# A two-layer trunk whose first tile after three norms is multiplied in float32 ahead of the norm's factor, and whose output is turned in the kernel

## The chip, the cores and the metric

The kernel runs on one core of a Trainium2 chip. A core has a matrix engine (TensorE, PE in the profile), a vector engine (VectorE, DVE), a scalar engine for activations, copies and casts (ScalarE, ACT), GpSimd (POOL), a queue engine that issues most DMAs (SyncE, SP), and 16 DMA engines. The engines run side by side, each in its own program order, and wait for each other by semaphores. Sums of matmuls stand in PSUM, eight buffers of 128 x 512 float32 here; everything else is in SBUF or, for weights and output, in HBM.

The metric is the device time of one execution in microseconds (us). A version has several executions, and its time is their median. The profile describes one further execution.

## The reference

A decoder trunk of two layers for 256 tokens (T) with 1024 features (D). Layer 0 mixes tokens by attention in three dilated windows, layer 1 by gated linear attention (GLA, in chunks of 64 tokens). Each is followed by a feed-forward part (FFN) with a causal convolution of width 3 and a gate. All of it is float32.

```
for i in range(DEPTH):
    mod = jax.nn.silu(c) @ w_ada[i] + b_ada[i]
    sh1, sc1, g1, sh2, sc2, g2 = [m[:, None, :] for m in jnp.split(mod, 6, axis=-1)]
    h = rmsnorm(x, norm_mix[i]) * (1.0 + sc1) + sh1
    if i % N_MIXERS == 0:
        y = dilated_mixture(h, w_in_a[j], w_out_a[j], rel_bias)
    else:
        y = gla_mixer(h, w_in_b[j], w_gate_b[j], b_gate_b[j], gnorm_b[j], w_out_b[j])
    x = x + g1 * y
    h = rmsnorm(x, norm_ffn[i]) * (1.0 + sc2) + sh2
    x = x + g2 * conv_ffn(h, w_up[i], conv_w[i], conv_b[i], w_down[i])
return rmsnorm(x, norm_final)
```

`rmsnorm(x, g)` is x times the inverse root of its mean square (over the features, plus 1e-6) times g. `conv_ffn` is u = h @ w_up, the convolution of u over the tokens, silu of one half times the other, and @ w_down. In `gla_mixer`, h @ w_in gives q, k, v, a low-rank input of the decay, and r, and the end is (rmsnorm(o, g_norm) * silu(r)) @ w_out.

Written for one token: h @ w = factor * ((x * a) @ w) + shift @ w, where a is the norm's weight times (1 + scale) and the factor is one number for each token.

## The kernel before

Activations lie with features on the partitions: `x` is eight tiles (kt = 0 to 7) of 128 features x 256 tokens. A weight matrix is used in tiles of 128 x 2048 float32, which is 256 output features for all eight kt, or another cut of that size.

**Split products.** A weight tile is loaded by SP into `raw` (four buffers), then `split` (L155) makes two float32r tiles of it: ACT casts it to `whi` (L165, two halves) and DVE subtracts that from `raw` into `wlo` (L168, two halves). Activations are split in the same manner. `mm3` (L171) is three matmuls in float32r, hi x hi (L174), hi x lo (L175) and lo x hi (L176). One tile of w_up, or of a gate, is 8 kt x 2 halves of features x 3 = 48 matmuls of 128x256.

**A norm.** As each tile of x is finished by `residual` (L271, DVE) at the end of a projection, `add_square` (L195) squares it on ACT and adds it to one of three partial sums, on POOL for kt 1 and 2 and else on DVE; kt 7 has a sum of its own. `rstd_of` (L183) sums over the partitions by a matmul with a matrix of 1/1024 (`ms`, L186, float32, three of them), then ACT takes Ln (L188) and Exp (L190): `r`, the factor, the same in all partitions. `all_normed` (L265) puts six small matmuls that nothing reads (`keep_warm`, L259) behind ms, and calls `normed` (L246) for each kt: DVE multiplies x by a and r (`xr`, L250), ACT adds the shift and casts (`hhi`, L252), DVE makes the rest (`hlo`, L253). `chain[kt]` keeps the last two instructions of kt; `chain[7]` those of the latest kt.

**Order.** A scheduler puts the instructions of each engine into one order when the program is built; `with behind(...)` says that what is inside is not issued before the instructions named. What runs on an engine is then fixed. A wait of one instruction holds everything behind it on its engine.

**PSUM.** `bank` (L72) hands out the eight buffers by three tags, p (2 buffers), s (3) and t (3). Without a tag it takes the next letter of `"pstpstst"`, round and round. A buffer is written again only after its readers are done.

**FFN** (L539): 22 tiles of w_up (`pab`, both halves of the gated pair in one buffer), convolution on ACT and DVE out of PSUM, and the split of the product; then w_down (`pd`). The split of tile 0 may begin from the sixth square on, that of tile 1 from `chain[3]` on, the others from `chain[7]`.

**GLA** (L592 to L781): norm, values (`pv`, L649 to L660), decay gates, then for each of four heads `states` (L671) and `output` (L716), and between the outputs the four gate tiles (`gate`, L741, matmuls `pr`), gate 0 ahead of the last output and gates 1 to 3 behind it. Then per head silu of the gate (L770), the product (L774), its split (`ohi` L776, `olo` L777), and `project` (L515, matmuls `py`).

```
    s3 = states(3)
    output(2, *s2)
    gate(0)
    next_ada()
    output(3, *s3)
    for n in range(1, 4):
        gate(n)
```

**The end** (L785 to L792): the last norm has no split. Its factor is multiplied into x by two multiplies on POOL and six on DVE, and four DMAs write 256 KB each, features on the partitions; the host turns the result.

**Modulation.** `next_ada` (L351) computes two of the 96 columns of shift, scale and gate at a time: a DMA of 1 MB, two dot products on DVE (L138). They are strewn over the program.

Of the kernel before, what the change touches and what calls it, by code (L numbers as in the profile page):

```python
# [57 lines left out]
def trunk(ctx: ExitStack, tc: tile.TileContext, I, out):  # L58
# [136 lines left out]
    def add_square(kt):  # L195

        sq = tmp.tile([P, T], F32, tag="sq", name="sq")
        i = nc.scalar.activation(sq, x[kt], AF.Square)
# [152 lines left out]
    def next_ada():  # L351
        if rest:
            ada_chunk(*rest.pop(0))
# [181 lines left out]
    project(I["w_out_a"], o, 0, 0)  # L535
    at_pool.__exit__(None, None, None)


    def ffn(l):  # L539
        h = all_normed(l, 1)  # L540
        with tc.tile_pool(name=f"ffn{l}", bufs=2) as pool:
            g_hi = [pool.tile([P, T], F32R, tag=f"ghi{i}", name="ghi", bufs=1) for i in range(NFF)]
            g_lo = [pool.tile([P, T], F32R, tag=f"glo{i}", name="glo", bufs=1) for i in range(NFF)]
            for i in range(NFF):
                with behind(*(squared[:1], chain[3], chain[7])[min(i, 2)]):
                    w = split(I["w_up"][l, i], 2048)
                pab = bank("pab")
                pu = [pab[:, :T], pab[:, T:]]
                for kt in range(KT):
                    for s in range(2):  # L550
                        mm3(pu[s][:, :T], parts(w, 2 * P * kt + P * s), h[kt], kt == 0 and s == 0, kt == KT - 1 and s == 1)
# [21 lines left out]
            exp_ln_after(silu)  # L573
            for f2 in range(0, KT, 2):
                pd = [bank("pd") for _ in range(2)]
                for half, f in ((0, 0), (0, 1), (1, 0), (1, 1)):
                    w = split(I["w_down"][l, f2 + f, half], 11 * P)
                    for j in range(11):
                        i = 11 * half + j
                        mm3(pd[f][:, :T], parts(w, P * j), (g_hi[i], g_lo[i]), i == 0, i == NFF - 1)  # L580
                for f in range(2):
                    residual(l, 1, f2 + f, pd[f][:, :T])
                    add_square(f2 + f)
                    if l == 1 and f2 + f < KT - 1:
# [4 lines left out]
    ffn(0)  # L589

# [11 lines left out]
    nc.gpsimd.memset(keep.rearrange("p (n c) -> p n c", c=CH)[:, :, 0:1], 0.0)  # L602
    h = all_normed(1, 0)

# [45 lines left out]
    for n in range(4):  # L650
        with behind(*(squared, chain[5], chain[7], glr_copy)[n]):
            w = split(I["w_v_b"][n], 2048)
            if n > 1:
                next_ada()
        for i in range(2):
            kt = 2 * n + i
            for t in range(2):
                ht = [y[:, P * t : P * t + P] for y in h[kt]]
                for s in range(2):
                    mm3(pv[t][s], ht, parts(w, D * i + 512 * s, 512), kt == 0, kt == KT - 1)  # L660
        if n == 1:
            e_q, e_k, e_d, dec = log_gates()
# [75 lines left out]

    r_g = []

    def gate(n):  # L741
        w = split(I["w_r_b"][n], 2048)
        pr = bank("pr", "p")
        for kt in range(KT):
            for s in range(2):
                mm3(pr[:, T * s : T * s + T], parts(w, 2 * P * kt + P * s), h[kt],
                    kt == 0 and s == 0, kt == KT - 1 and s == 1)
        if n % 2 == 0:
            r_g.append(gt([P, 4, T], "r4", tag=("C", "cs")[n // 2]))
        nc.scalar.copy(r_g[-1][:, 2 * (n % 2) : 2 * (n % 2) + 2, :], pr.rearrange("p (a b) -> p a b", a=2))  # L750

# [6 lines left out]
    output(2, *s2)  # L758
    gate(0)
    next_ada()  # L760
    output(3, *s3)
    for n in range(1, 4):
        gate(n)
        if n < 2:
            next_ada()
    o = []
    for n in range(4):
        r = r_g[n // 2][:, 2 * (n % 2) : 2 * (n % 2) + 2, :]
        with behind(*norm_ops):
# [9 lines left out]
    exp_ln_after(last_hi)  # L779
    project(I["w_out_b"], o, 1, 0)  # L780
    gl_pool.__exit__(None, None, None)  # L781

    ffn(1)

    r = rstd_of([sums[0], sums[1], sums[2]])  # L785
    for kt in range(2):
        nc.gpsimd.tensor_tensor(x[kt], x[kt], r, op=ALU.mult)
    for kt in range(2, KT - 1):
        nc.vector.tensor_tensor(x[kt], x[kt], r, op=ALU.mult)
    nc.vector.scalar_tensor_tensor(x[7], x[7], col(C_NFIN + 7), r, op0=ALU.mult, op1=ALU.mult)  # L790
    for eng, a, b in ((nc.sync, 2, 4), (nc.scalar, 0, 2), (nc.sync, 4, 6), (nc.sync, 6, 8)):
        eng.dma_start(out[a:b].rearrange("k p t -> p k t"), x_all[:, a:b, :])  # L792

# [77 lines left out]
def build(arrays):  # L871
    import concourse.bacc as bacc

    nc = bacc.Bacc("TRN2", target_bir_lowering=False, num_devices=1)
# [4 lines left out]
    out = nc.dram_tensor("out_y", (KT, P, T), F32, kind="ExternalOutput").ap()  # L879
    with tile.TileContext(nc, schedule_with_timeline_sim=True) as tc:  # L880
# [12 lines left out]
```

## Time and profile before

| | us |
|---|---|
| median of three runs | 809.89 |
| the runs | 803.45, 811.63, 809.89 |
| the profiled execution | 807.78 |
| its span on the engines | 806.1 |
| PE busy in it | 782.4 |
| DVE busy in it | 645.4 |
| ACT busy in it | 466.5 |
| mean granted clock of PE in it | 0.993 |

The span is the time from the first to the last instruction; the 1.7 us beside it lie around the program. Rows of the timeline have the start in us from the span's start, the length (of several instructions of one kind in a row together), engine, line, operation, output<-inputs by the program's names, their shape and count, and in brackets how long the engine had been idle and what ended that. The length of a matmul includes its way through the array, so matmuls overlap, and the distance of their starts is what one costs in a stream. A float32 matmul shows as two records, a float32r one as one.

### The profile page before, as it was taken

What the parts mean: (1) busy time and instruction counts of PE and PEld (TensorE: products, weight loads), DVE (VectorE), ACT (ScalarE), POOL (GpSimd) and SP (SyncE); (2) the same over time, 40 slices, a digit from 0 to 9 for tenths busy, and PEclk for the clock granted to TensorE, in tenths of its full rate; (3) what the DMA queues carried; (4) which work ended last, traced back from release to release, by engine and by line L of the source; (5) the groups of instructions that cost most, each with busy time, mean ns of one, the idle gap of its engine ahead of it and who ended that gap; (6) DMA issues with size and microseconds to landing.
All of it is one profiled execution on the core that took longest, in us unless ns stands there. A gap on an engine that the chain in (4) does not pass through costs nothing.

```text
span 806.1 us, 15899 instructions
## 1 busy us (share of the span) xinstructions
PE 782.4 (97%) x6464; PEld 752.5 (93%) x6464; DVE 645.4 (80%) x1153; ACT 466.5 (58%) x867; POOL 16.8 (2%) x42
## 2 busy tenths in 40 slices
PE   8999999999999989999999999999999999999995
PEld 6899999999999889999999998889998999999995
DVE  6998977879778769999997877776468999987552
ACT  5566555455545547777766445644556866766551
POOL 1000000000000010000000000000010000000100
PEclk9999999999999999999999999999999999999998
DMA  8998668486596736877647884873343776644521
GB/s 343 416 328 320 225 256 309 164 305 237 205 321 224 262 105 215 313 257 261 222 136 244 285 322 151 327 261 105 105 159 107 281 274 237 252 145 146 188 99 52
DMA packets 32694, 184.70 MB, mean 229 GB/s; under 512 B 5804, under 2 KB 8364, under 8 KB 15982
## 3 DMA queue, kind: packets, MB, share of 16 engines
q1 hardware_dynamic: 32350, 183.44, 63.1%
q8 instruction: 50, 0.82, 0.4%
q10 hardware_dynamic: 272, 0.26, 0.1%
q14 instruction: 22, 0.18, 0.1%
HBM read 182.59 MB, written 1.10 MB: 228 GB/s over the span
## 4 chain that ended last, share of the span: by engine, by line
PE 67%; DVE 14%; DMA 11%; ACT 4%; issue 2%; DVEq 0%; SPq 0%; ACTq 0%
PE pab L176 10%; PE pab L174 10%; PE pab L175 10%; DVE wlo L168 6%; DMA raw<-in_wqk 5%; PE pd L176 4%; PE pd L175 4%; PE pd L174 4%; PE pqk L176 3%; PE pqk L175 3%; PE pqk L174 3%; DMA raw<-in_wv 2%; DVE ada_raw L138 2%; PE py L175 2%; PE py L174 2%
## 5 line engine op out<-in xcount | busy, mean ns | idle before, releaser
L168 DVE TENSOR_TENSOR wlo<-raw,whi 128x1024 fp32r<-128x1024 f32 (+2 forms) x274 | 295.3, 1106 | 56.9 <-ACT whi L165 56.0
L165 ACT CAST whi<-raw 128x1024 fp32r<-128x1024 f32 (+2 forms) x274 | 247.9, 953 | 153.9 <-PE pab L175 50.5
L174 PE MATMUL pab<-hhi,whi 128*128 128x256 f32 x704 | 194.1, 277 | 1.5 <-ACT hhi L252 1.5
L175 PE MATMUL pab<-hlo,whi 128*128 128x256 f32 x704 | 193.9, 276 | 0.5 <-DVE hlo L253 0.5
L176 PE MATMUL pab<-hhi,wlo 128*128 128x256 f32 x704 | 194.0, 276 | 0.4 <-DVE wlo L168 0.4
L174 PEld LDWEIGHTS pab<-hhi,whi 128*128 128x128 f32 x704 | 132.0, 188 | 2.2 <-ACT hhi L252 1.9
L175 PEld LDWEIGHTS pab<-hlo,whi 128*128 128x128 f32 x704 | 132.0, 188 | 0.9 <-DVE hlo L253 0.9
L176 PEld LDWEIGHTS pab<-hhi,wlo 128*128 128x128 f32 x704 | 132.0, 188 | 0.8 <-DVE wlo L168 0.8
L174 PE MATMUL pqk<-hhi,whi 128*128 128x256 f32 x448 | 123.5, 287 | 3.0 <-ACT hhi L252 2.3
L175 PE MATMUL pqk<-hlo,whi 128*128 128x256 f32 x448 | 125.6, 284 | 0.5 <-DVE hlo L253 0.5
L176 PE MATMUL pqk<-hhi,wlo 128*128 128x256 f32 x448 | 125.0, 283 | 0.0
L138 DVE CUSTOM_DVE_ANT_0 ada_raw<-ada_raw,c_bc 128x1024 f32<-128x1024 f32 x96 | 114.1, 1224 | 5.1 <-DMA ada_raw<-in_w_ada 5.0
L176 PE MATMUL pd<-ghi,wlo 128*128 128x256 f32 x352 | 98.0, 280 | 1.5 <-DVE wlo L168 1.5
L175 PE MATMUL pd<-glo,whi 128*128 128x256 f32 x352 | 98.1, 280 | 0.0
L174 PE MATMUL pd<-ghi,whi 128*128 128x256 f32 x352 | 97.7, 279 | 0.0
L174 PEld LDWEIGHTS pqk<-hhi,whi 128*128 128x128 f32 x448 | 83.7, 191 | 4.7 <-ACT hhi L252 2.7
L175 PEld LDWEIGHTS pqk<-hlo,whi 128*128 128x128 f32 x448 | 85.4, 191 | 1.0 <-DVE hlo L253 0.7
L176 PEld LDWEIGHTS pqk<-hhi,wlo 128*128 128x128 f32 x448 | 85.1, 191 | 0.2
L176 PEld LDWEIGHTS pd<-ghi,wlo 128*128 128x128 f32 x352 | 65.8, 187 | 1.7 <-DVE wlo L168 1.7
L175 PEld LDWEIGHTS pd<-glo,whi 128*128 128x128 f32 x352 | 66.0, 188 | 0.0
L174 PEld LDWEIGHTS pd<-ghi,whi 128*128 128x128 f32 x352 | 65.9, 188 | 0.0
L558 ACT ACTIVATE r<-pab,small 128x256 f32<-128x256 f32 x88 | 48.5, 559 | 11.7 <-DVE r L561 11.3
(176 smaller groups left out, 1247.0 us busy)
## 6 DMA issues: line engine op xcount, KB each, us to landing
ada_raw<-in_w_ada SPq DMA_DIRECT2D x47, 1024.0 KB, 6.5
raw<-in_w_up SPq DMA_DIRECT2D x44, 1024.0 KB, 5.1
raw<-in_w_down SPq DMA_DIRECT2D x32, 704.0 KB, 4.2
raw<-in_wqk SPq DMA_DIRECT2D x18, 1024.0 KB, 7.0
raw<-in_wv SPq DMA_DIRECT2D x14, 768.0 KB, 4.6
raw<-in_w SPq DMA_DIRECT2D x7, 960.0 KB, 6.6
raw<-in_w_out_a SPq DMA_DIRECT2D x4, 1024.0 KB, 6.4
raw<-in_w_v_b SPq DMA_DIRECT2D x4, 1024.0 KB, 5.7
```

Of the source, the lines that this page charges most:

```text
L138: nc.vector.tensor_tensor_reduce(w, w, c_bc, op0=ALU.mult, op1=ALU.add, scale=1.0, scalar=0.0, accum_out=dot,)
L165: copied[0] = nc.scalar.copy(hi[:, c], raw[:, c])
L168: last_lo[0] = nc.vector.tensor_tensor(lo[:, c], raw[:, c], hi[:, c].bitcast(F32), op=ALU.subtract)
L174: mm(ps, a[0], b[0], start=start, stop=False)
L175: mm(ps, a[0], b[1], start=False, stop=False)
L176: return mm(ps, a[1], b[0], start=False, stop=stop)
L558: nc.scalar.activation(r, u[:, :T], AF.Identity, scale=cw[2], bias=col(C_CB + 44 * l + f))
```

## The change

For three of the norms (ahead of both FFNs and of GLA) the tile of weights that came first, or in GLA the tile of gate 0, is not split. It is multiplied in float32 with `early_x` = x times a, which needs no factor. A 257th column of `early_x` holds the shift, so that shift @ w comes out in the 257th column of the sums. Four of the sixteen products (kt 0 and 1) stand ahead of `ms`, twelve behind it, in the place of the small matmuls. When the factor is there, `whole` makes the finished tile of the sums: ACT copies the 257th column, DVE multiplies by the factor, ACT adds the column.

In the FFN, tile 0 of w_up thus has no matmuls of its own; `whole` stands behind `chain[5]`, the split of tile 1 may begin from `chain[0]`, that of tile 2 from `chain[5]`. In GLA gate 0 is made at the norm and kept; gate 1 takes the place that gate 0 had ahead of the last output, and gates 2 and 3 stand behind it. The early sums are in two buffers with tag p in the FFNs and with tag t in GLA. The new instructions are 48 float32 matmuls of 128x257, 24 scalings of x and 24 copies of one column on ACT, and for each of the three tiles two small copies, two multiplies and two additions; 144 split matmuls and three splits go.

At the end, x is turned by 16 transposes on PE into four buffers, the mean square is taken with tokens on the partitions (128 x 4 numbers), the factor is applied by two scalings on ACT and two on DVE out of PSUM, and four DMAs write 128 x 512 each, tokens on the partitions. The host no longer turns the result. A smaller scratch for DMA descriptors makes room in SBUF.

```diff
@@ add_square, norms
-            (nc.gpsimd if kt < 3 else nc.vector).tensor_tensor(acc, sums[part], sq, op=ALU.add)
+            last_sum[:] = [(nc.gpsimd if kt < 3 else nc.vector).tensor_tensor(acc, sums[part], sq, op=ALU.add)]
-    def all_normed(l, sub):
-        r = rstd_of([sums[0], sums[1], sums[2]])
+    early_x = [state.tile([P, T + 16], F32, tag=f"ex{k}", name="early_x") for k in range(KT)]
+    def shift_columns(l, sub):
+        with behind(*chain[7]):
+            for kt in range(KT):
+                nc.scalar.copy(early_x[kt][:, T : T + 1], mod[l, 3 * sub, kt])
+    def scale(l, sub, kt):
+        return nc.scalar.mul(early_x[kt][:, 0:T], x[kt], mod[l, 3 * sub + 1, kt][:, 0:1])
+    def load_early(src):
+        early = wraw.tile([P, 2048], F32, tag="raw", name="raw")
+        nc.sync.dma_start(early, src)
+        return early
+    def all_normed(l, sub, tag, early):
+        ps = [bank("early", tag) for _ in range(2)]
+        def products(tiles):
+            for kt in tiles:
+                for s in range(2):
+                    mm(ps[s][:, 0 : T + 1], early[:, 2 * P * kt + P * s : 2 * P * kt + P * s + P], early_x[kt][:, 0 : T + 1],
+                       start=(kt == 0), stop=(kt == KT - 1))
+        products(range(2))
+        r = rstd_of([sums[0], sums[1], sums[2]], tag="t" if tag == "p" else "s")
         with behind(norm_ops[0]):
-            keep_warm(6)
-        return [normed(l, sub, r, kt) for kt in range(KT)]
+            products(range(2, KT))
+        def whole(s, out):
+            dot = tmp.tile([P, 1], F32, tag="dot", name="dot", bufs=4)
+            nc.scalar.copy(dot, ps[s][:, T : T + 1])
+            nc.vector.tensor_tensor(out, ps[s][:, 0:T], r, op=ALU.mult)
+            nc.scalar.activation(out, out, AF.Identity, bias=dot[:, 0:1])
+            return out
+        return [normed(l, sub, r, kt) for kt in range(KT)], whole
     def residual(l, sub, kt, ps):
-        i = nc.vector.scalar_tensor_tensor(x[kt], ps, g[:, 0:1], x[kt], op0=ALU.mult, op1=ALU.add)
+        with behind(*(last_sum if kt == 7 else ())):
+            i = nc.vector.scalar_tensor_tensor(x[kt], ps, g[:, 0:1], x[kt], op0=ALU.mult, op1=ALU.add)
@@ project (and likewise at w_down of the first FFN, with w_r_b[0])
+        shift_columns(l, 1)
...
+            if n == 3:
+                early = load_early(I["w_up"][l, 0])
             for i in range(2):
                 residual(l, sub, 2 * n + i, ps[i][:, T * i : T * i + T])
                 add_square(2 * n + i)
+                scale(l, 1, 2 * n + i)
@@ ffn
-                with behind(*(squared[:1], chain[3], chain[7])[min(i, 2)]):
-                    w = split(I["w_up"][l, i], 2048)
-                pab = bank("pab")
-                pu = [pab[:, :T], pab[:, T:]]
-                for kt in range(KT):
+                if i == 0:
+                    with behind(*chain[5]):
+                        pu = [whole(s, pool.tile([P, T], F32, tag="u", name="u")) for s in range(2)]
+                else:
+                    with behind(*((), chain[0], chain[5], chain[7])[min(i, 3)]):
+                        w = split(I["w_up"][l, i], 2048)
+                    pab = bank("pab")
+                    pu = [pab[:, :T], pab[:, T:]]
+                for kt in range(KT if i else 0):
@@ GLA
-        with behind(*(squared, chain[5], chain[7], glr_copy)[n]):
+        with behind(*(chain[0], chain[5], chain[7], glr_copy)[n]):
             w = split(I["w_v_b"][n], 2048)
...
+        if n == 0:
+            with behind(*chain[5]):
+                r_g = [gt([P, 2, T], "r2")]
+                for s in range(2):
+                    whole(s, r_g[0][:, s, :])
...
-    gate(0)
+    gate(1)
     next_ada()
     output(3, *s3)
-    for n in range(1, 4):
+    for n in range(2, 4):
         gate(n)
@@ the end
-    r = rstd_of([sums[0], sums[1], sums[2]])
-    for kt in range(2):
-        nc.gpsimd.tensor_tensor(x[kt], x[kt], r, op=ALU.mult)
-    for kt in range(2, KT - 1):
-        nc.vector.tensor_tensor(x[kt], x[kt], r, op=ALU.mult)
-    nc.vector.scalar_tensor_tensor(x[7], x[7], col(C_NFIN + 7), r, op0=ALU.mult, op1=ALU.mult)
-    for eng, a, b in ((nc.sync, 2, 4), (nc.scalar, 0, 2), (nc.sync, 4, 6), (nc.sync, 6, 8)):
-        eng.dma_start(out[a:b].rearrange("k p t -> p k t"), x_all[:, a:b, :])
+    halves = [slice(P * t, P * t + P) for t in range(2)]
+    y_ps = [[bank("y") for _ in range(2)] for _ in halves]
+    ps = bank("ms")
+    nc.vector.tensor_scalar(x[7], x[7], col(C_NFIN + 7), None, op0=ALU.mult)
...
+    for half in range(2):
+        for t, own in enumerate(halves):
+            c = slice(512 * half, 512 * half + 512)
+            d = y[:, D * t : D * t + D][:, c]
+            if t:
+                nc.vector.tensor_scalar(d, y_ps[t][half], r[:, 2:3], None, op0=ALU.mult)
+            else:
+                nc.scalar.mul(d, y_ps[t][half], r[:, 0:1])
+            nc.sync.dma_start(out[own, c], d)
```

Where the mean square of the end is taken, partial sums 0 and 1 go first, then the transposes of kt 0 and 1, then partial sum 2 (kt 7), then the other transposes.

More of the change, by code (lines that the diff above doesn't have):

```diff
@@ L587, in ffn @@
                         next_ada()
-    ffn(0)
+        return early
+    early = ffn(0, early)
     gl_pool = tc.tile_pool(name="gla", bufs=1)
@@ L602, in trunk @@
     nc.gpsimd.memset(keep.rearrange("p (n c) -> p n c", c=CH)[:, :, 0:1], 0.0)
-    h = all_normed(1, 0)
+    h, whole = all_normed(1, 0, "t", early)
     causal = gt([P, 2, P], "causal")
@@ L767, in trunk @@
     for n in range(4):
[L768 removed]
+        r = r_g[n]
         with behind(*norm_ops):
@@ L779, in trunk, with turned, mean_square @@
     exp_ln_after(last_hi)
-    project(I["w_out_b"], o, 1, 0)
+    early = project(I["w_out_b"], o, 1, 0)
     gl_pool.__exit__(None, None, None)
-    ffn(1)
-    r = rstd_of([sums[0], sums[1], sums[2]])
-    for kt in range(2):
-        nc.gpsimd.tensor_tensor(x[kt], x[kt], r, op=ALU.mult)
-    for kt in range(2, KT - 1):
-        nc.vector.tensor_tensor(x[kt], x[kt], r, op=ALU.mult)
-    nc.vector.scalar_tensor_tensor(x[7], x[7], col(C_NFIN + 7), r, op0=ALU.mult, op1=ALU.mult)
-    for eng, a, b in ((nc.sync, 2, 4), (nc.scalar, 0, 2), (nc.sync, 4, 6), (nc.sync, 6, 8)):
-        eng.dma_start(out[a:b].rearrange("k p t -> p k t"), x_all[:, a:b, :])
+    ffn(1, early)
+    halves = [slice(P * t, P * t + P) for t in range(2)]
+    y_ps = [[bank("y") for _ in range(2)] for _ in halves]
+    ps = bank("ms")
+    nc.vector.tensor_scalar(x[7], x[7], col(C_NFIN + 7), None, op0=ALU.mult)
+    def turned(tiles):
+        for kt in tiles:
+            for t, own in enumerate(halves):
+                i = nc.tensor.transpose(y_ps[t][kt // 4][:, P * (kt % 4) : P * (kt % 4) + P], x[kt][:, own], ident)
+        return i
+    def mean_square(parts):
+        for part in parts:
+            for t, own in enumerate(halves):
+                i = mm(ps[:, 2 * t : 2 * t + 2], sums[part][:, own], ones_d[:, 0:2], start=(part == t == 0), stop=(part == 2 and t == 1))
+        return i
+    with behind(last_pd[0]):
+        last = mean_square(range(2))
+    with behind(last):
+        last = turned(range(2))
+    with behind(last):
+        last = mean_square([2])
+    with behind(last):
+        turned(range(2, KT))
+    ln = tmp.tile([P, 4], F32, tag="m", name="ln")
+    nc.scalar.activation(ln, ps[:, 0:4], AF.Ln, bias=eps[:, 0:1])
+    r = tmp.tile([P, 4], F32, tag="m", name="rstd")
+    nc.scalar.activation(r, ln, AF.Exp, scale=-0.5)
+    y = wspl.tile([P, 2048], F32, tag="whi", name="y")
+    for half in range(2):
+        for t, own in enumerate(halves):
+            c = slice(512 * half, 512 * half + 512)
[5 more added lines that the diff above has]
+            nc.sync.dma_start(out[own, c], d)
 def _bias_onehot():
@@ L878, in build @@
     }
-    out = nc.dram_tensor("out_y", (KT, P, T), F32, kind="ExternalOutput").ap()
+    out = nc.dram_tensor("out_y", (T, D), F32, kind="ExternalOutput").ap()
     with tile.TileContext(nc, schedule_with_timeline_sim=True) as tc:
```

30 lines of the change are left out of this document (19 added, 11 removed).

## The prediction

> **What bounds the kernel now.** I read the page first: totals of the engines, then the slices with the granted clock. After that the timeline of TensorE (PE) around each norm, beside VectorE's (DVE) and ScalarE's (ACT), and last a table of stretches with the clock in each.
>
> ```profile
> span 806.1 us, 15899 instructions
> PE 782.4 (97%) x6464; PEld 752.5 (93%) x6464; DVE 645.4 (80%) x1153; ACT 466.5 (58%) x867; POOL 16.8 (2%) x42
> PEclk9999999999999999999999999999999999999998
> ```
>
> PE is busy for 97% of the span: time goes down only by less PE work or by fewer holes in it. The places touched are three norms, the gates and the end. The first of the norms, on PE then in tables of the products pab and of one clean tile (columns: bounds, length, PE busy (count), PEld, DVE, ACT, in the second POOL, granted clock, DMA share, GB/s), last the weight loads of ms (ns, least/median/most):
>
> ```profile
> 297.83 0.28 PE L176 MATMUL py<-ohi,wlo 128*128 128x256 f32 x1
> 297.95 1.02 PE L186 MATMUL ms<-sqacc,ones_d 128*128 128x256 f32 x4
> 299.20 0.70 PE L186 MATMUL ms<-sq,ones_d 128*128 128x256 f32 x2 [0.22 <-ACT sq L198]
> 299.73 1.50 PE L263 MATMUL warm<-ones_d 128*128 128x128 f32 x12
> 301.97 0.38 PE L174 MATMUL pab<-hhi,whi 128*128 128x256 f32 x1 [0.74 <-ACT hhi L252]
> 302.62 0.38 PE L175 MATMUL pab<-hlo,whi 128*128 128x256 f32 x1 [0.26 <-DVE hlo L253]
> 301.97:314.19 12.22, 11.77 (x96) 11.21 (x97) 0.00 (x0) 0.00 (x0) 1.00 0.32 97
> 308.76:314.20 5.44, 5.44 (x50) 5.44 (x49) 4.86 (x9) 3.91 (x6) 0.00 (x0) 1.00 0.62 206
> L186 PEld LDWEIGHTS ms<-sqacc,ones_d x16: 187/189/192, 297.8 to 796.7; 128*128 128x128 f32 x16
> ```
>
> I write L for the start of the first ms instruction (297.95), which is the end of the out-projection's issue. Then 96 products, the first two tiles of w_up, run from L + 4.02 to L + 16.25, and tile 2 starts there. The clean tile has 48 starts in 5.44 us (of the 50 in the row two still run from ahead of it), 0.113 each, at a clock of 1.00. The 1.02 us of ms are four records for two float32 instructions; with a last one as long as 0.38, three pitches make 0.64: 0.213 a record, 0.43 us an instruction of float32 with 256 columns. What the norm's chain does on ACT and DVE in that time:
>
> ```profile
> 299.93 0.47 ACT L188 ACTIVATE ln<-ms,eps 128x256 f32<-128x256 f32 x1 [0.79 <-PE ms L186]
> 300.44 0.42 ACT L190 ACTIVATE rstd<-ln 128x256 f32<-128x256 f32 x1
> 300.89 1.28 DVE L250 SCALAR_TENSOR_TENSOR xr<-x_all,mod,rstd 128x256 f32<-128x256 f32 x3 [2.26 <-ACT rstd L190]
> 304.87 1.23 DVE L168 TENSOR_TENSOR wlo<-raw,whi 128x1024 fp32r<-128x1024 f32 x1
> 306.01 0.48 DVE L250 SCALAR_TENSOR_TENSOR xr<-x_all,mod,rstd 128x256 f32<-128x256 f32 x1
> ```
>
> From the last ms (299.20) to rstd's end and the first xr it is 1.69 us. DVE then takes 0.40 us for each xr or hlo of 128x256 ((1.28 - 0.48) / 2) and 1.14 for each half of a wlo (306.01 - 304.87). The norm before the other FFN is the same to 0.01 us:
>
> ```profile
> 609.00 1.02 PE L186 MATMUL ms<-sqacc,ones_d 128*128 128x256 f32 x4
> 613.67 0.38 PE L175 MATMUL pab<-hlo,whi 128*128 128x256 f32 x1 [0.26 <-DVE hlo L253]
> ```
>
> **The two FFN norms.** Removed from each: 48 split products (5.44 us), the warm matmuls, and of the split 2 ACT casts and 2 DVE subtractions. Added: 16 float32 products with 257 columns. The trace shows none of these; the nearest row is ms with 256 columns and a fixed weight tile, 0.43 us (below, if the width and changing weights cost nothing, 0.43; above, with a weight load of 0.19 a record laid bare, 0.81). I take 0.43, as ms too has a weight load for each record, and hides it. So 16 x 0.43 = 6.9 us: PE work grows by 1.4 us, against a hole of L to L + 4.02 that it is to fill.
>
> The order after: 4 products (1.72), 3 ms (1.29), 12 products. Products end at L + 3.01 + 5.16 = L + 8.17. The last ms starts at L + 2.58 instead of L + 1.25, so the first xr, which I call T, comes at L + 2.58 + 1.6 = L + 4.2 (0.1 less than 1.69, as its records no longer wait for sq). If PE could go on at L + 8.17 with tile 1, tile 2 would start at L + 13.6: 2.6 us won.
>
> It can't, by the instruction order of the changed program. Tile 1's sums (pab) get the same PSUM buffer of tag p as the first half of the early sums, in both FFN norms: its first matmul waits for the DVE multiply that reads those sums. That multiply stands on DVE behind 7 xr, 6 hlo and 2 halves of wlo: 13 x 0.40 + 2 x 1.14 = 7.5 us, and it takes 0.4 itself: done at T + 7.9 = L + 12.1. PE stands from L + 8.17 to L + 12.1, 3.9 us, with nothing in it (the warm matmuls are gone). Behind the waiting matmul stands all of tile 1 and everything later on PE. Tile 1 then takes 5.44: tile 2 at L + 17.6 against L + 16.25. **+1.4 us for each of the two, +2.8.** Late next would be hlo of kt 6, another multiply, an xr and a wlo later: T + 11.5, needed at about T + 12. So that stays covered, by half a us.
>
> **The GLA norm.** The first tile is here gate 0, which before ran last. PSUM buffers of pv aren't those of the early sums, so nothing stands.
>
> ```profile
> 486.95 1.02 PE L186 MATMUL ms<-sqacc,ones_d 128*128 128x256 f32 x4
> 490.91 0.50 PE L174 MATMUL pv<-whi,hhi 128*128 128x512 f32 x1 [0.73 <-ACT hhi L252]
> 491.25 0.39 PE L175 MATMUL pv<-wlo,hhi 128*128 128x512 f32 x1
> ```
>
> pv began 3.96 us after ms (and the next 0.34 later, not 0.23, which makes 4.07); now it begins when the products are done, 8.17 after it. +4.1 us, to be paid back where gate 0 was. There, before (first PE, then a table of the matmuls pr alone, then ACT, then DVE):
>
> ```profile
> 578.65 0.59 PE L186 MATMUL ms<-oacc,ones_d 128*128 128x256 f32 x2
> 585.68 0.28 PE L174 MATMUL py<-ohi,whi 128*128 128x256 f32 x1
> 586.40 0.38 PE L175 MATMUL py<-olo,whi 128*128 128x256 f32 x1 [0.44 <-DVE olo L777]
> 578.85:585.40 6.55, 6.50 (x54) 6.50 (x55) 0.58 (x1) 1.00 0.01 3
> 581.52 1.16 ACT L770 ACTIVATE r<-r 128x512 f32<-128x512 f32 x2
> 582.58 1.99 ACT L165 CAST whi<-raw 128x1024 fp32r<-128x1024 f32 x2
> 584.94 1.33 ACT L776 CAST ohi<-on 128x256 fp32r<-128x256 f32 x4
> 583.65 2.36 DVE L168 TENSOR_TENSOR wlo<-raw,whi 128x1024 fp32r<-128x1024 f32 x2
> 585.93 1.43 DVE L777 TENSOR_TENSOR olo<-on,ohi 128x256 fp32r<-128x256 f32 x4
> ```
>
> I write M for the last ms (578.65). Between it and py 56 matmuls pr lie on PE (578.90 to 585.68, 0.118 each; 54 of them start before 585.40), and under them runs a chain: silu, whi, wlo, ohi, olo, and at M + 7.75 py flows. Removing 48 pr takes 5.7 us of PE work from behind M, as the program's order leaves 8 pr there, done at M + 1.4. But the chain is as long as before: py's second matmul needs olo, which in the changed order stands behind the same wlo, and this behind a whi with one more silu (1.16 / 2, some 0.53 in pitch) ahead of it. So py flows at M + 8.3. PE stands for about 6 us, **and gate 0's removal gives -5.7 + 6.2 = +0.5: with the front +4.6 us.** The bounds of this: had the chain been cut as well, 4.1 - 5.7 = -1.6; had olo slipped behind one more half of a wlo (2.36 / 2), +5.8.
>
> **The clock.** A hole in PE may cost more than itself. The trace has one place (two matmul rows, then a table of three stretches, columns as above with POOL behind ACT):
>
> ```profile
> 529.27 0.28 PE L176 MATMUL pqk<-hhi,wlo 128*128 128x256 f32 x1
> 530.99 0.44 PE L688 MATMUL kdt<-ident,k_d 128*128 128x128 f32 x2 [1.44 <-DVE k_d L680]
> 528.90:532.36 3.46, 1.79 (x14) 1.35 (x13) 3.46 (x8) 2.73 (x5) 0.00 (x0) 1.00 0.89 310
> 532.36:535.77 3.41, 3.41 (x18) 3.19 (x18) 3.41 (x5) 0.00 (x0) 0.00 (x0) 0.50 0.75 312
> 535.80:539.20 3.40, 3.40 (x29) 3.02 (x28) 2.80 (x7) 1.21 (x4) 0.00 (x0) 1.00 1.03 333
> ```
>
> After a hole of 1.44 us and sparse small matmuls the clock was 0.50 for 3.41 us, and PE did 18 records where the next stretch has 29: 3.41 x (1 - 18/29) = 1.3 us lost. At the norms of before, with the warm matmuls in them, it stayed at 1.00. After the change two holes of 3.9 and one of 6 us stand bare. I count on a fall where three quarters of a stretch of 3.41 us, at a chance place, lie in the hole. In the long hole that is certain; in one of 3.9 us the stretch may start from 0.86 ahead of the hole to 1.35 inside it, 2.2 of 3.41, two in three. A small part of the slow stretch falls into the hole itself, so 1.2 each: 2 x 2/3 x 1.2 + 1.2 = **+2.8 us** (0 with no fall; 5 with three, each at half speed throughout, 1.7).
>
> The Trainium skill, "TensorE: Matmul & The Clock Gate", Part 1: The HAM clock gate, speaks against the change: it says that the clock falls to half after an idle window of about 3.4 us, windows that run freely. Taken to the letter it asks for a window that is wholly idle; the row above shows a fall after a window that was busy for 1.79 of 3.46 us. By the letter a hole of 3.9 us holds a whole window only once in about seven ((3.9 - 3.41) / 3.41), and the sum would be 1.3 us lower.
>
> **The end.** Removed: eight multiplies of 128x256 on POOL and DVE, and the wait of the output DMAs for them.
>
> ```profile
> 796.25 1.03 PE L186 MATMUL ms<-sqacc,ones_d 128*128 128x256 f32 x4
> 798.18 0.47 ACT L188 ACTIVATE ln<-ms,eps 128x256 f32<-128x256 f32 x1 [0.79 <-PE ms L186]
> 799.13 2.82 DVE L789 TENSOR_TENSOR x_all<-x_all,rstd 128x256 f32<-128x256 f32 x5 [2.19 <-ACT rstd L190]
> 800.45 2.30 SPq L792 DMA_DIRECT2D out_y<-x_all  x3
> ```
>
> With E = 796.25 the span ends at E + 9.83; the last of the DMAs is issued by 802.75, E + 6.5, and 3.3 us later all is over. After: ln at about E + 2.0 as now (it waits for x of kt 7 and its square), but on 128x4, so below 0.47 and 0.42 with the Exp: E + 2.6. The 16 transposes are no longer than those of k_d (0.22 a record): 12 behind the last ms, done by about E + 3.1 to 4.6. Two scalings on ACT beside two on DVE, each about the 0.58 of a 128x512 silu: DMAs from E + 3.3, the last issued at about E + 4.9, the end at E + 8.2. **-1.6 us** (0 if the transposes come late, -2.5 if ln and Exp shrink to nothing).
>
> **What costs nothing.** 24 scalings of x and 24 copies on ACT (0.42 each or less) lie in the out-projection and w_down, where ACT has nothing but casts: it is 58% busy; without that cover the products of kt 6 and 7 wait one such step, 0.4 us a norm. u's two multiplies and additions add 0.8 us of DVE work an FFN where 2.3 of wlo go. The early load takes a place of four in raw until L + 8.2; the loads of tiles 1 to 3 are in the others, and the split of tile 1 frees its own at T + 4.3, the same time. SP's queue: one more kind of load, ahead in the order as tile 0's was.
>
> **Sum.** 2.8 + 4.6 + 2.8 - 1.6 = +8.6 us on the profiled execution of 807.78 us (span 806.1): 816.4. The three runs have their median at 809.89 (803.45 to 811.63), so the profiled one is in their midst, 2.1 below the median; I stay with it: 816.5.
>
> **Rivals.** *The clock holds.* Holes as forecast, but no fall at the FFN norms, or none at all: 807.78 + 5.8 to + 7.3 = 813.6 to 815. For it: where the stretches lie is chance. Against it: the row of 0.50. Chance 0.17. The rule of the skill's page comes out inside this rival, at about 815.
> *The buffer is free in time (not slower).* If DVE multiplies the early sums by T + 4 instead of T + 7.9 (its queue running through ahead of the products), PE goes on at L + 8.17, each FFN wins 2.6, and 4.6 - 5.2 - 1.6 = -2.2 gives 805.6; it decides from a multiply done before L + 8.2. If the chain ahead of py were shorter too, -1.6 instead of 4.6: 799.4. For it: the change fills a hole that is really there, 4.02 us by three. Against: 7.5 us of DVE steps are queued ahead, each with its row. Chances 0.07 and 0.06.
> *Float32 products dearer.* Width 257 and new weights at 0.55 us rather than 0.43: in the FFN norms the hole takes it up (1.9 of the 3.9), in GLA's it doesn't: +2, and with the clock falling at every hole and later DVE steps late by their half us, 820 to 825. Chance 0.14.
>
> **How the numbers follow.** Forecast as worked out, 814 to 820: 0.56; the rivals as said. The range of 8 in 10 takes in the first rival and the near ones of both sides: 805 to 822. About 1% (8.1 us) is what a measurement here can tell from no change: 801.8 to 818.0 around the median, 799.7 to 815.9 around the profiled run. Forecast lies just at that edge. Faster by over 1%: 0.07. Slower by over 1%: half or more of the forecast's 0.56, the dear case 0.14, a little of the first rival: 0.48. Within: 0.45.
>
> **What would show it.** In the profile after: early products 0.43 us apart by two records; at the first pab of both FFN norms an idle of about 4 us put down to DVE, the multiply u; ahead of py an idle of about 6 us put down to ACT ohi or DVE olo; a clock of 0.50 for 3.4 us behind these holes; pv 8.2 us after ms; the span ending 8.2 us after the last pd. No idle ahead of pab, or a short one ahead of py, would make the forecast wrong.

## The result and the profile after

The changed kernel takes 816.41 us, the median of seven executions (813.06 to 819.1), against 809.89 before: a ratio of 1.0114 with a 95% interval from 1.0077 to 1.015. A ratio, here and below, is an estimate from the fast runs (one slow run, of the experiment on buffer and order, is left out) and not the quotient of the two medians, which is 1.0081 here. Its profiled execution took 813.71 us. From the page of that profile, the span with its instructions, PE's total and the slices of the granted clock:

```profile
span 811.9 us, 15803 instructions
PE 785.3 (97%) x6402; PEld 755.1 (93%) x6402; DVE 639.0 (79%) x1150; ACT 474.0 (58%) x922; POOL 14.2 (2%) x40
PEclk9999999999999999999999999999998999999999
```

PE runs 62 records fewer and is busy for 2.9 us more: 785.3 against 782.4. So its busy time did not shrink, though some of it is matmuls at half clock (below), and the span grew by 5.8 us. The view of PE's waits (engine, line, waited for; total, times, longest) names two new ones at its head:

```profile
PE pab L174 <- DVE u L302: 7.6, 2, 3.8
PE py L174 <- ACT ohi L835: 5.7, 1, 5.7
```

These are the holes at the two FFN norms and ahead of the GLA output projection. Around the first of them, PE and then DVE on the timeline:

```profile
297.22 1.47 PE L291 MATMUL early<-early_x,raw 128*128 128x257 f32 x6
298.52 1.03 PE L186 MATMUL ms<-sqacc,ones_d 128*128 128x256 f32 x4
299.82 5.36 PE L291 MATMUL early<-early_x,raw 128*128 128x257 f32 x24
308.99 0.56 PE L174 MATMUL pab<-hhi,whi 128*128 128x256 f32 x1 [3.81 <-DVE u L302]
300.97 1.27 DVE L250 SCALAR_TENSOR_TENSOR xr<-x_all,mod,rstd 128x256 f32<-128x256 f32 x3 [3.07 <-ACT rstd L190]
308.52 0.74 DVE L302 TENSOR_TENSOR u<-early,rstd 128x256 f32<-128x256 f32 x2
```

PE has done the early products at 305 and does nothing until DVE, which began the norm at 300.97, comes to the multiply at 308.52. Then the clock. These are stretches behind the three holes (bounds, length, PE, PEld, DVE, ACT, POOL, granted clock, DMA share, GB/s):

```profile
308.99:312.40 3.41, 3.41 (x16) 3.41 (x17) 3.41 (x6) 3.41 (x8) 0.00 (x0) 0.51 0.79 332
588.98:592.35 3.37, 3.35 (x14) 3.06 (x15) 3.32 (x9) 2.36 (x8) 0.00 (x0) 0.50 0.41 134
624.86:629.95 5.09, 5.09 (x24) 5.09 (x25) 5.09 (x9) 5.09 (x10) 0.00 (x0) 0.50 0.77 278
```

PE issues 14 to 24 records where at full clock some 30 to 45 fit. In GLA, the early products, the first pv, and further on ACT, DVE and PE ahead of py:

```profile
487.23 1.89 PE L291 MATMUL early<-early_x,raw 128*128 128x257 f32 x8
495.27 0.58 PE L174 MATMUL pv<-whi,hhi 128*128 128x512 f32 x1
584.59 1.67 ACT L829 ACTIVATE r<-r 128x512 f32<-128x512 f32 x3
587.27 2.35 DVE L168 TENSOR_TENSOR wlo<-raw,whi 128x1024 fp32r<-128x1024 f32 x2
588.98 1.01 PE L174 MATMUL py<-ohi,whi 128*128 128x256 f32 x3 [5.72 <-ACT ohi L835]
590.01 0.58 PE L175 MATMUL py<-olo,whi 128*128 128x256 f32 x1
```

pv begins 8.15 us after the last pd (487.12) instead of 4.07, and the chain of silu (now three in a row), split and olo ends half a us later than before: the matmul that waits for the first olo starts 8.29 us after the last ms (581.72), before 7.75. The end, on PE, ACT and SP's queue:

```profile
803.76 0.95 PE L859 MATMUL ms<-ones_d,sqacc 128*128 128x2 f32 x8
805.60 0.26 ACT L871 ACTIVATE ln<-ms,eps 128x4 f32<-128x4 f32 x1 [0.70 <-PE ms L859]
806.13 1.41 ACT L882 ACTIVATE y<-y,rstd 128x512 f32<-128x512 f32 x2
806.85 1.81 SPq L883 DMA_DIRECT2D out_y<-y  x4
```

The span of 811.93 ends 8.2 us after the first of these. Stage by stage, from the starts of PE's records at each border (us; the third column is a second profile of the changed kernel, taken with the experiments):

| stage | before | after | after, again | after - before |
|---|---|---|---|---|
| to the end of the attention's out-projection | 297.83 | 297.10 | 297.34 | -0.73 |
| FFN 0: norm and w_up | 125.17 | 127.85 | 127.85 | +2.68 |
| FFN 0: w_down | 63.84 | 62.17 | 62.17 | -1.67 |
| GLA, with its norm | 122.05 | 125.42 | 125.59 | +3.37 |
| FFN 1: norm and w_up | 125.17 | 129.03 | 129.19 | +3.86 |
| FFN 1: w_down | 62.07 | 62.07 | 62.07 | 0 |
| the end | 9.95 | 8.29 | 8.29 | -1.66 |
| span | 806.08 | 811.93 | 812.50 | +5.85 |

In FFN 0 one float32 product already runs among the last matmuls of the projection, so its norm and w_up cost 0.4 us more than the row says, and the row above it 0.4 less.

### The profile page after: what moved, and what is told of

Same layout as the page of the kernel before. It is cut to its first block, busy times and chain, and to the rows that moved or that the text cites. A ratio compares the mean times of both kernels' runs of the same rounds, so it can differ in the third digit from the quotient of the medians.

```text
span 811.9 us, 15803 instructions
## 1 busy us (share of the span) xinstructions
PE 785.3 (97%) x6402; PEld 755.1 (93%) x6402; DVE 639.0 (79%) x1150; ACT 474.0 (58%) x922; POOL 14.2 (2%) x40
## 3 DMA queue, kind: packets, MB, share of 16 engines
q1 hardware_dynamic: 32110, 183.70, 62.9%
## 4 chain that ended last, share of the span: by engine, by line
PE 65%; DVE 15%; DMA 11%; ACT 6%; issue 3%; SPq 0%; ACTq 0%; DVEq 0%
PE pab L174 10%; PE pab L176 10%; PE pab L175 10%; DVE wlo L168 6%; PE pd L175 5%; PE pd L174 5%; PE pd L176 5%; DMA raw<-in_wqk 4%; PE pqk L176 2%; DMA raw<-in_wv 2%; PE pqk L175 2%; PE pqk L174 2%; ACT whi L165 2%; PE py L174 2%; DVE ada_raw L138 2%
## 5 line engine op out<-in xcount | busy, mean ns | idle before, releaser
L165 ACT CAST whi<-raw 128x1024 fp32r<-128x1024 f32 (+2 forms) x268 | 241.9, 952 | 160.6 <-PE pab L175 60.3
L168 DVE TENSOR_TENSOR wlo<-raw,whi 128x1024 fp32r<-128x1024 f32 (+2 forms) x268 | 287.2, 1103 | 60.8 <-ACT whi L165 60.0
L174 PE MATMUL pab<-hhi,whi 128*128 128x256 f32 x672 | 187.7, 279 | 7.6 <-DVE u L302 7.6
L175 PE MATMUL pab<-hlo,whi 128*128 128x256 f32 x672 | 187.2, 279 | 0.0
L176 PE MATMUL pab<-hhi,wlo 128*128 128x256 f32 x672 | 187.1, 278 | 0.0
L174 PEld LDWEIGHTS pab<-hhi,whi 128*128 128x128 f32 x672 | 128.0, 191 | 8.4 <-DVE u L302 8.4
L175 PEld LDWEIGHTS pab<-hlo,whi 128*128 128x128 f32 x672 | 128.1, 191 | 0.0
L176 PEld LDWEIGHTS pab<-hhi,wlo 128*128 128x128 f32 x672 | 128.0, 190 | 0.0
L607 ACT ACTIVATE r<-pab,small 128x256 f32<-128x256 f32 x84 | 45.7, 557 | 7.8 <-DVE r L610 7.8
```

Source lines behind the costliest of these rows:

```text
L165: copied[0] = nc.scalar.copy(hi[:, c], raw[:, c])
L168: last_lo[0] = nc.vector.tensor_tensor(lo[:, c], raw[:, c], hi[:, c].bitcast(F32), op=ALU.subtract)
L174: mm(ps, a[0], b[0], start=start, stop=False)
L175: mm(ps, a[0], b[1], start=False, stop=False)
L176: return mm(ps, a[1], b[0], start=False, stop=stop)
L607: nc.scalar.activation(r, u[:, :T], AF.Identity, scale=cw[2], bias=col(C_CB + 44 * l + f))
```

## The experiments

Eight kernels were run in two groups, each group on one chip with executions of the kernel before among its own; a ratio is to these (median 810.51 us in the first group, 806.0 in the second).

**Another buffer for tile 1's sums** (in both FFNs of the changed kernel; its own round of tags goes on as it was):

```diff
-                    pab = bank("pab")
+                    tag = next(cycle)
+                    pab = bank("pab", "s" if i == 1 else tag)
```

> The changed kernel with one edit: in both FFNs the sums of tile 1 stand in a buffer of tag s, so that they no longer share one with the early sums. Theory (the buffer holds PE, and behind it the order on DVE): the idle of 3.8 us ahead of the first pab goes, but hlo of kt 6 still stands behind both multiplies u, an xr and two halves of a wlo, done about 11.2 us after the first xr, so tile 1 ends at 12.6 us after it instead of 13.3 and the slow clock: a hole of 2 to 3 us appears inside tile 1. 816.4 less 1.5 to 5: 811.5 to 815. Rival (the buffer alone is the cost): tile 1 runs through, 3.4 us and the slow clock saved in each FFN: about 806. Rival (the float32 products are the cost): no change, 816.

Measured: 811.22 us, ratio 1.0009 (0.9976 to 1.0042); the interval of the changed kernel lies wholly above it. The first matmul of tile 1, and the longest wait inside the tile:

```profile
306.28 0.47 PE L174 MATMUL pab<-hhi,whi 128*128 128x256 f32 x1
311.87 0.39 PE L174 MATMUL pab<-hhi,whi 128*128 128x256 f32 x1 [0.40 <-ACT hhi L252]
```

The wait for the multiply is gone, as is the slow clock behind it. The hole of 2 to 3 us inside the tile didn't come as one: the scheduler put matmuls of tile 2 ahead of tile 1's products of kt 6 and 7 (36 matmuls use up kt 0 to 5 of tile 1; the 38th, at 311.19, reads an hlo 2 us before DVE makes that of kt 6, at 313.30). But tile 1 doesn't run through either. By its first 48 matmuls w_up is 1.7 us behind a stream without breaks, through several short waits, and 1.7 us is what the slow clock costs the changed kernel in this place: from the first pab to the last both take 115.85 us. FFN 0's norm and w_up take 123.69 us, 4.2 less than in the changed kernel, which is the hole and nothing else. The ratio is 0.0105 or 8.5 us below the changed kernel's, more than the theory's 1.5 to 5 and less than the rival's 10. So the buffer is most of the cost, and the second bound behind it is there, with 1.7 us instead of 2 to 3.

**Buffer and order** (tiles 1 and 2 in other buffers; tile 2's subtraction behind the last hlo; the multiplies u behind it):

```diff
-            for i in range(NFF):
+            for i in (1, 2, 0) + tuple(range(3, NFF)):
                 if i == 0:
-                    with behind(*chain[5]):
+                    with behind(last_lo[0]):
...
-                        w = split(I["w_up"][l, i], 2048)
-                    pab = bank("pab")
+                        w = split(I["w_up"][l, i], 2048, lo_after=chain[7] if i == 2 else ())
+                    tag = next(cycle)
+                    pab = bank("pab", {1: "s", 2: "t"}.get(i) or tag)
```

> The changed kernel with two edits in both FFNs: tiles 1 and 2 have their sums in buffers of tags s and t, and the multiplies of the early sums and tile 2's subtraction stand behind the last hlo on DVE. Theory: no wait of over 1 us from the early products to tile 2, which begins 13.6 us after the out-projection's end (before 16.25, changed kernel about 17.5 and slow clock); no slow clock there. Each FFN wins 3.4 us and 1.7 to 2.5 of clock on the changed kernel: 816.4 - 10.5 = 806. Rival (DVE is the bound of the whole FFN, so that what is won at its head is lost in it): 812 to 816, with waits for wlo later.

Measured: 810.46 us, ratio 0.9982 (0.9947 to 1.0017), 0.013 below the changed kernel, as the theory had it, though not at 806, as the kernel before stood at 810.51 in this group. But FFN 0's norm and w_up take 123.72 us, and the experiment without the new order took 123.69. The order on DVE adds nothing; the 1.7 us that tile 1 loses to waits are in both (their matmuls of w_up in FFN 0 take 115.89 and 115.85 us), and behind them w_up runs on without a break, so DVE is no bound of the rest.

**Small matmuls in the holes** (16 behind the early products of each FFN norm, 24 ahead of py):

```diff
+        if tag == "p":
+            with behind(e):
+                warmed[0] = keep_warm(16, "t")
...
+    with behind(last_pr[0]):
+        warmed[0] = keep_warm(24, "t")
...
```

The first matmuls of tile 1 and of py are put behind these.

> The changed kernel with its holes filled: 16 small matmuls that nothing reads behind the early products of both FFN norms, 24 ahead of py. Every wait stays. Theory (the clock's fall is a cost of its own): clock of 1.00 behind all three holes, and 1.5 + 2.5 + 1.7 us less: 810.7. Rival (only the holes cost; the slow stretches are covered by waits for DVE): 815 to 817 with a clock of 1.00. Rival (the filler is in the way, PE being late for py): above 816.

Measured: 811.0 us, ratio 1.0007 (0.9981 to 1.0034). The first hole, filled, the clock behind it and behind the one at FFN 1, and the filler ahead of py, with the first olo on DVE:

```profile
304.29 3.73 PE L263 MATMUL warm<-ones_d 128*128 128x128 f32 x32
308.27 0.39 PE L174 MATMUL pab<-hhi,whi 128*128 128x256 f32 x1 [0.24 <-DVE u L307]
308.27:312.00 3.73, 3.73 (x32) 3.73 (x33) 3.73 (x7) 3.73 (x8) 0.00 (x0) 1.00 0.78 325
620.11:625.00 4.89, 4.89 (x41) 4.89 (x42) 4.89 (x9) 4.89 (x10) 0.00 (x0) 1.00 0.77 275
580.77 5.52 PE L263 MATMUL warm<-ones_d 128*128 128x128 f32 x48
582.12 0.76 DVE L846 TENSOR_TENSOR olo<-on,ohi 128x256 fp32r<-128x256 f32 x2
```

pab still starts 4 us after the early products, but at a clock of 1.00: 32 records in 3.7 us, where the changed kernel had 16 in 3.4. By stages this is worth 1.6 us in FFN 0 (126.26 against 127.85) and in FFN 1 some 2.4 (131.14 against 129.03, but at a slower pace of all its 1008 matmuls, 0.1178 us for 0.1133, which makes 4.5; told of below). GLA is 2.5 shorter (122.87 against 125.42), but that is not the clock alone. The scheduler made another order here, with 51 gate matmuls behind the last ms where the changed kernel has 8, so not every wait stayed: two olo are done at 582.9, and what holds the start of py until 586.04 is the filler, as the last rival feared, though the time is not its 816. The projection by itself takes 21.75 us, against 23.56 in the changed kernel, 1.8 less. Together 5.8 us: the fall of the clock is a cost of its own.

**Three gates in the kernel before** (gate 0's load, split and matmuls left out; head 0 takes gate 1's result, by one more copy on DVE):

```diff
...
-    gate(0)
+    gate(1)
     next_ada()
     output(3, *s3)
-    for n in range(1, 4):
+    for n in range(2, 4):
...
```

> The kernel before, with the tile of gate 0 left out (its load, split and 48 matmuls); head 0 takes gate 1's result. Theory (the chain from the last norm factor through silu, the split and olo is the bound, gate 0 only lay over it): a hole of 5.5 to 6 us ahead of py and a slow clock behind it; 0 to 2.5 us slower than before, 810 to 812.5, though 5.6 us of PE work are gone. Rival (PE work is time): 804.

Measured: 813.34 us, ratio 1.0022 (0.9985 to 1.0058), by itself not to be told from 1: between 1.2 us faster and 4.7 slower, which holds the theory's 0 to 2.5 and not the rival's 6 faster. The first py, and a stretch behind it:

```profile
589.49 0.80 PE L174 MATMUL py<-ohi,whi 128*128 128x256 f32 x2 [5.72 <-ACT ohi L778]
589.49:593.50 4.01, 3.98 (x17) 3.69 (x18) 3.88 (x11) 2.98 (x9) 0.00 (x0) 0.50 0.50 184
```

A tile of 48 matmuls is gone and the GLA stage takes 123.85 us, 1.8 more than with it (both profiles have one slow stretch near the first transposes of the states, and the same pace in py). The hole is the same 5.72 us as in the changed kernel, though this kernel has no early product. What gate 0 did in this place was to lie over the chain and to keep the clock up.

**The changed kernel again**, unedited.

> The changed kernel itself, to stand beside the next three and to see how far its profile repeats. All theories: the same three holes (3.8, 3.8 and 5.7 us) with a clock of 0.50 behind each, a ratio of 1.007 to 1.015. On the pace of w_up (0.113 us a matmul in both FFNs of the first two profiles, 0.118 in one or both FFNs of the four experiments): if the pace hangs on the program, it is 0.113 in both here; if it hangs on the execution, 0.118 may come up, 5 us for an FFN, and the runs of one kernel then lie in heaps some 5 us apart.

Measured: 814.8 us, ratio 1.0125 (1.0094 to 1.0155). The same waits to a tenth of a us (the stages stand in the table above):

```profile
PE pab L174 <- DVE u L302: 7.6, 2, 3.8
PE py L174 <- ACT ohi L835: 5.7, 1, 5.7
```

The pace of w_up was 0.113 in both FFNs, which speaks neither for nor against the execution.

**GLA as before in the changed kernel** (its norm with split tiles and small matmuls, gate 0 back ahead of the last output; the FFNs and the end changed):

```diff
...
-    h, whole = all_normed(1, 0, "t", early)
+    h = split_norm(1, 0)
...
-    gate(1)
+    gate(0)
     next_ada()
     output(3, *s3)
-    for n in range(2, 4):
+    for n in range(1, 4):
...
```

> The changed kernel with GLA's norm and gates as before (small matmuls behind ms, four split gates, gate 0 ahead of the last output); the FFNs and the end stay changed. Theory (an early gate costs 4.1 us at the norm and gives nothing back, the chain ahead of py being the bound): pv 4.0 us after ms, no hole ahead of py, 4.3 us and the clock of 1.5 less than the changed kernel, a ratio 0.007 below it. Rival (a gate ahead saves its work later): 0 to 1.5 us more than the changed kernel, as 48 split matmuls come back for 16 float32 ones.

Measured: 806.89 us, ratio 1.0000 (0.9972 to 1.0028), 0.0125 below the changed kernel where 0.007 was expected. Its waits, and where FFN 1's tile 1 starts:

```profile
PE pab L174 <- DVE u L302: 3.8, 1, 3.8
614.84 0.47 PE L174 MATMUL pab<-hhi,whi 128*128 128x256 f32 x1
```

The edit did more than was meant. GLA's old norm takes two buffers from the round, so that in FFN 1 tile 1 no longer meets the early sums: its hole is gone, and FFN 1's norm and w_up take 124.13 us instead of 129.03. GLA alone is 120.33 against 125.42, 5.1 less, of the 5.8 that the theory gave it (4.3 and 1.5); with the projection's matmuls counted at one pace (0.1178 us here, 0.1133 there) it is 5.9. The rival, by which gate 0 back would cost up to 1.5, is out.

**The end alone**, on the kernel before (the last hunk of the change and what it needs).

> The kernel before with the new end alone. Theory: the span ends 8.2 us after the last pd instead of 9.9, all else as before: 1.7 us faster, 0.998. Rival (part of that gain is the early scalings ahead of it, or the DMAs come out as late): 0 to 0.5 us.

Measured: 804.05 us, ratio 0.9986 (0.9958 to 1.0014): by itself not to be told from 1. Its profile has the end at 8.29 us after the last pd, as in the changed kernel, against 9.95 before; the DMAs are issued from 3.1 us after the first ms (792.54) on:

```profile
795.62 1.81 SPq L825 DMA_DIRECT2D out_y<-y  x4
```

**Buffer, gates and end**: early products in the FFNs only, tile 1's sums in a buffer of tag s, GLA as before, the new end.

> What the experiments so far speak for: early products in the FFNs with tile 1's sums in a buffer of tag s, GLA as before, the new end. Theory: each FFN's head 1.0 to 1.5 us shorter than before (tile 2 at 14.9 us after the out-projection's last ms would start, instead of 16.25), the end 1.7: 4 us faster than before, 0.995. Rival (hardly any gain beyond the end, as holes of half a us remain in tile 1 and DVE has the two multiplies more): 0.998.

Measured: 800.36 us, ratio 0.9948 (0.9923 to 0.9974), as the theory had it: half a per cent faster than the kernel before, and further below the changed one. Tile 1 in FFN 0, and what is left of waits at pab:

```profile
305.60 0.47 PE L174 MATMUL pab<-hhi,whi 128*128 128x256 f32 x1
PE pab L174 <- ACT hhi L252: 0.8, 2, 0.4
```

The norm and w_up take 123.69 and 124.13 us against 125.17 twice (with the early product that sits in the projection, a gain of 1.05 each), the end 8.28 against 9.95; 3.8 us together. Tile 1 still loses 1.7 us to waits.

## Why the prediction held

**The float32 products.** Forecast at 0.43 us each, with 0.81 as the upper bound. 24 records in 5.36 us, the last as long as a record of 0.39, are 0.216 a record, 0.432 a product, where ms had 0.213 a record; width 257 and new weights cost next to nothing. The rival of dearer products is out.

**The buffer at the FFN norms.** Forecast was a hole of 3.9 us at both, put down to the multiply u. Measured 3.81 at both. The first experiment shows the cause: with another buffer, and nothing else, it goes. The wait on the buffer is the step that carried the sign: without it the time can't be told from before (ratio 1.0009). The next bound that the forecast named (hlo of kt 6, covered by half a us) stayed covered as forecast: in the third experiment, at full clock, the 1008 matmuls of FFN 0 run from first to last in 114.25 us, which is 0.1135 each. Only where the wait on the buffer is gone do the waits behind it show, with 1.7 us.

**The GLA norm and gate 0.** Forecast was +4.1 in front and +0.5 behind. pv starts 4.08 us later. py flows at 590.01, 8.29 us after the last ms (581.72), forecast 8.3; before it was 7.75. The three-gate experiment shows that the chain and not the gates' work set this place.

**The clock.** This term was too small. Forecast were 2.8 us, from two chances in three for a fall at each FFN's hole, a certain one ahead of py, and 1.2 us for each. It fell at all three, in both profiles of the changed kernel, and at FFN 1 and py the slow time was twice as long (623.1 to 629.9, 585.5 to 592.4, each beginning inside the hole; 3.4 at FFN 0). At full clock the same matmuls took 1.6, 2.4 and 1.8 us less, 5.8 in all. The forecast's condition for a fall, three quarters of a stretch without work, was too strict as well. The two stretches of 3.41 us on either side of the fall at FFN 1, whose hole lasts from 621.04 to 624.86:

```profile
619.67:623.08 3.41, 1.37 (x7) 0.86 (x5) 3.41 (x7) 1.45 (x5) 0.00 (x0) 1.00 0.22 43
623.08:626.49 3.41, 1.64 (x7) 1.64 (x8) 3.41 (x8) 3.41 (x8) 0.00 (x0) 0.50 1.01 428
```

The clock fell after a stretch in which PE had been busy for 1.37 us of 3.41, and stayed low after one with 1.64. In "TensorE: Matmul & The Clock Gate", Part 1: The HAM clock gate, the Trainium skill gives an idle window of about 3.4 us as the condition. The slow stretches of 3.4 and 6.8 us agree with windows of that length; that a wholly idle one is needed does not agree, as the first of these rows shows, and as a fall came at ten of ten holes of 3.8 to 5.7 us in all profiles, where by that a hole of 3.8 us would bring one in eight or nine cases ((3.81 - 3.41) / 3.41, an estimate). How much work in a stretch keeps the clock up stays open.

**The end.** Forecast -1.6, measured -1.66, and the same in the kernel that has this part alone.

**What was not forecast.** The slow stretch at 532 us of the kernel before is missing in both profiles of the changed one, and so is 1.67 us between the first transposes of the states and the last ms (46.2 us for 47.9). It came in three of the ten profiles (before, the second and the fourth experiment), so it is no doing of the change. FFN 0's w_down is 1.67 us shorter: the kernel before has a wait of PE for wlo 21 us after the stage's start, and the changed one has not. In the profiles where PE waits for u at that FFN's norm (after, twice, the third and the sixth experiment) the stage takes 62.2 to 62.3 us; without one 62.9 to 63.8, but for the last experiment, whose w_down ran at another pace for two thirds of its length. That DVE gets ahead while PE waits is the likely reason; it was not tried.

**The total.** Stage by stage, forecast and measured: the two FFN heads +4.4 and +7.0 (with the product that runs in the projection), GLA +5.8 and +3.4, the end -1.6 and -1.7, FFN 0's w_down 0 and -1.7, the part up to the end of the attention's out-projection 0 and -1.2 (the product taken out); together +8.6 and +5.85. Of what GLA lacks, 1.7 us are the slow stretch at 532 and 0.8 the pace of the projection's matmuls (0.1178 us before, 0.1133 after; see the last section). The border that ends the first part lies between 296.4 and 298.6 us in the ten profiles, so its 1.2 us say nothing of the change. That 816.5 stands beside 816.41 is therefore luck in part: the forecast was 8.6 us on top of a profiled execution 2.1 us below its median, and the medians differ by 6.5 us, in the second group by 8.8. What held are the sign, the three holes with their lengths and causes, and the end; the clock was put at half of what it cost.

## What to carry to other kernels

Work that is moved into a hole has to have its result read before the next user of its buffer: ask of each PSUM buffer who frees it, and what stands ahead of that reader on its engine. Work that is moved away is missed where it was: if a chain of small steps ran under it, the chain stays and the hole shows. And a hole on PE of 3.8 us or more cost here its length and 1.6 to 2.4 us more through the halved clock, so a filler that nothing reads was worth its place at the FFN norms, as long as it ends before the work that waits is ready; ahead of py it didn't.

## What the runs showed of the hardware that was not expected

A whole stage of w_up ran at one of two paces, at a granted clock of 1.00 in both. From the kernel before and the three-gate kernel, two stretches of 10 us in the w_up of each FFN (the first pair is the kernel before):

```profile
340.00:350.00 10.00, 10.00 (x90) 10.00 (x90) 8.66 (x17) 7.46 (x13) 0.00 (x0) 1.00 0.80 293
640.00:650.00 10.00, 10.00 (x91) 10.00 (x90) 10.00 (x17) 6.62 (x13) 0.00 (x0) 1.00 0.65 232
```

```profile
340.00:350.00 10.00, 10.00 (x87) 10.00 (x87) 9.08 (x18) 6.21 (x11) 0.00 (x0) 1.00 0.81 292
640.00:650.00 10.00, 10.00 (x87) 10.00 (x86) 9.26 (x18) 8.35 (x16) 0.00 (x0) 1.00 0.51 160
```

Over the whole stage, behind the waits at its head, the starts are 0.1133 us apart in the one and 0.1178 in the other, without a wait between, which is 4.7 us for a w_up of 1056 matmuls. In FFN 0 the order of PE's instructions is the same in these two kernels. The first three experiments had 0.1178 in FFN 1 (and 0.1133 in FFN 0), the three-gate kernel 0.1178 in both, and the other six profiles 0.1133 in both. These four are all profiles of the first group, on one chip, and none of the second group, on another, is among them, so the chip may have a part in it. The 35 runs of the kernel before in the first group lie in heaps at about that distance: 3 from 804.8 to 806.3, 21 from 807.9 to 812.0 and 11 from 813.4 to 816.3 us; of the 24 in the second, 21 lie from 802.6 to 808.4 and 3 from 812.9 to 814.0. That points to the execution and not to the program alone.

Both paces occur in every profile, though. w_down ran at 0.1178 in both FFNs of all of them (its 528 matmuls take 62.07 us where nothing waits), except in FFN 0 of the last experiment: there the distance goes from 0.1178 to 0.1133 at the one wait of PE in the stage, of 1.0 us, and stays so. The same wait in the first experiment brought no change. And py ran at 0.1178 in the kernel before and at 0.1133 in the changed one. So the pace holds through a stream and can change at a break; what sets it stays open. It is why w_up is compared here only after its matmuls have been counted at one pace, and why a difference of 1% between two single runs of this kernel tells nothing.
